# Attention two heads at a time, spread over the gate layer's blocks

## The chip, the cores and the metric

The kernel runs on one core of one Trainium2 chip. The time is device microseconds of one launch. The core has five engines with a queue each: TensorE (PE, matmuls; its weight loads are listed as PEld), VectorE (DVE), ScalarE (ACT), GpSimd (POOL) and SyncE (SP), which issues most of the DMAs. SBUF holds the tiles; matmuls write to PSUM, which has eight banks of 128 partitions x 512 fp32 values.

## What is computed

The reference is two blocks of a network over 512 positions of 1024 channels, one after the other. The first block mixes by spatial gating, a depthwise convolution and a pooling branch, and is not touched. The second block projects its normed input `h` to the inputs of two branches and two gates:

```python
proj = h @ w_in
qa, ka, va, za, ba, aa, qb, kb, vb, ga, gb = split(proj)
oa = gated_delta_rule(conv(qa), conv(ka), conv(va), ...)     # 4 heads of 128
ob = chunk_band_attention(qb, kb, vb, rel_bias)              # 8 heads of 64
mix = sigmoid(ga) * (oa @ w_branch_a) + sigmoid(gb) * (ob @ w_branch_b)
x = x + mix @ w_out
```

Attention is causal by chunks of 64 positions, with a bias by distance: for a head, `softmax(q @ k.T / 8 + bias) @ v`, where a query block of 128 positions sees its own block and those before it. So query blocks 0 to 3 have scores of 128 x 128, 256, 384 and 512.

## The kernel before

**Layout.** Activations stand transposed, channels on partitions and 512 positions along the row. A layer's weights come in blocks of 128 output channels, 512 KB each. `prep` (L149) loads a block on SP's queue and splits it into a high and a low part (`whi` by ACT, `wlo` by DVE); every product of a layer is three matmuls of 512 columns (`mm3`, L168 to L170), so a block of 1024 input channels takes 24. These are in a format that takes one pass. The small matmuls of attention and of the delta rule are plain fp32 and show as two instructions each in the trace, called passes here; transpositions show as one.

**Order.** `step` (L243) puts work in a list and `emit` (L246) issues it in that order, with weight blocks prepared two steps ahead. That is the order of the code, not of the engines: a planner (the tile framework) orders the instructions of each engine when the program is built. It goes through the program with a cost model of its own, and of what is ready by that model it sends first what stands first in the code; work from further down fills the time in which earlier work waits. Buffers are rings by tag: a tile waits until one of its ring's buffers is free. On the chip each engine then takes its list in order.

**The stage of the change** has PSUM banks "mm" 2, "g0" 2, "g1" 2 and "att" 2 (L766). Its steps, in the order of the code: the layer `w_za`, small gates, two delta-rule heads (`gdn_steps(0)` and `(1)`: three blocks of `w_qkv` each, then `gdn_first` and `gdn_second`), eight blocks of `w_qkb` (the attention's queries and keys, L1123), `w_vb` (its values, L1124), `step(attention)` (L1125), two more delta-rule heads (L1126, L1127), and 16 blocks of `w_gab`, the gate layer (L1128), whose results go to DRAM. After it `branches` (L1151) needs the outputs of all heads.

**Attention** goes over 8 heads, and in a head over three groups of query blocks, (0, 1), (2) and (3): 24 groups in one step. A tile of `S["at"]` holds two heads, the even one in partitions 0 to 63, the odd one in 64 to 127; `pr` is a head's half. `scores` (L1053) loads the head's bias in its first group, multiplies queries by keys with 64 rows of contraction (L1062) into one "att" bank, and makes the softmax on DVE and ACT in a tile `z` from the ring "az" of two. `values` (L1073) works on the group before: it transposes `z` by PE (L1080) into an "att" bank, copies that to a tile of the ring "ap" (two), multiplies by `vb` (L1086) into a third "att" tile, in the head's half of the output partitions, and copies the half to `ao`. When a pair of heads is complete, `ao` is split for the branches. The ring "g" of nine buffers (L854) holds query, key and value tiles of delta-rule heads, three a head, and later gate tiles.

Of the kernel before, what the change touches and what calls it, by code (L numbers as in the profile page):

```python
# [12 lines left out]
ALU = mybir.AluOpType  # L13
AX = mybir.AxisListType

P = 128
T = 512
D = 1024
NB = 8
NT = 4  # L20
# [6 lines left out]
DH_SCALE = 64 ** -0.5  # L27
# [16 lines left out]
def build(tc, d, out):  # L44
    nc = tc.nc
# [3 lines left out]
    pe = nc.tensor  # L49
# [8 lines left out]
    S = {}  # L58
# [26 lines left out]
    def blk(pool, tag, bufs, dt=F32, shape=(P, T)):  # L85
        return pool.tile(list(shape), dt, tag=tag, bufs=bufs, name=tag)
# [18 lines left out]
    def auxps(tag=None):  # L105
        tag = tag or PS["aux"]
        return PS["pool"].tile([P, T], F32, tag=tag, bufs=PS["banks"][tag], name=tag)
# [4 lines left out]
    def acopy(o, i, scale=1.0):  # L112
        act.activation(out=o, in_=i, func=AF.Copy, scale=scale)  # L113

    def tt(o, a, b, op):
        dve.tensor_tensor(out=o, in0=a, in1=b, op=op)  # L116

    def ts(o, a, s1, s2, op0, op1=None):
        if op1 is None:
            dve.tensor_scalar(out=o, in0=a, scalar1=s1, scalar2=None, op0=op0)  # L120
        else:
            dve.tensor_scalar(out=o, in0=a, scalar1=s1, scalar2=s2, op0=op0, op1=op1)

    def stt(o, a, s, b, op0, op1):
        dve.scalar_tensor_tensor(out=o, in0=a, scalar=s, in1=b, op0=op0, op1=op1)  # L125

    def split(src, hi, lo):
        acopy(hi, src)
        tt(lo, src, hi.bitcast(F32), ALU.subtract)
# [5 lines left out]
    def pair(set_):  # L135
        if set_ == "A":
            return blk(acts, "xh", 8, F32R), blk(acts, "xl", 8, F32R)
        return blk(acts, "th", 8, F32R), blk(acts, "tl", 8, F32R)
# [28 lines left out]
    def mm3(ps, wh, wl, xh, xl, first, last):  # L167
        pe.matmul(ps, wh, xh, start=first, stop=False)  # L168
        pe.matmul(ps, wh, xl, start=False, stop=False)  # L169
        pe.matmul(ps, wl, xh, start=False, stop=last)  # L170
# [72 lines left out]
    def step(fn, chunk=None, bg=2400, hold=None):  # L243
        steps.append((chunk, fn, bg, hold))
# [26 lines left out]
    def kchunks(kb):  # L271
        kmax = 8 if kb <= 8 else -(-kb // (-(-kb // 8)))
        return [(k0, min(kb, k0 + kmax)) for k0 in range(0, kb, kmax)]

    def linear(name, nbs, kb, xs, consume, bg=2400, tag="mm"):

        for n in nbs:
            st = {}
            for k0, k1 in kchunks(kb):
                def fn(wh, wl, n=n, k0=k0, k1=k1, st=st):  # L280
                    if k0 == 0:
                        st["ps"] = auxps(tag)
                    for k in range(k0, k1):
                        xh, xl = xs(k)
                        w = slice((k - k0) * P, (k - k0 + 1) * P)
                        mm3(st["ps"], wh[:, w], wl[:, w], xh, xl, k == 0, k == kb - 1)
                    if k1 == kb:
                        consume(n, st["ps"], ALL)

                step(fn, d[name][n][:, k0 * P:k1 * P], bg)  # L290
# [32 lines left out]
    def linear_tm(name, halves, kb, xs, consume, tag2, between=None):  # L323

        for hf in halves:
            st = {}
            cuts = [0, 1] if between is not None and hf == 0 else [0]
            cuts += list(range(2, kb + 1, 2))
            for k0, k1 in zip(cuts, cuts[1:]):
                def fn(wh, wl, hf=hf, k0=k0, k1=k1, st=st):  # L330
                    if k0 == 0:
                        st["ps"] = [mmps(), mmps(), auxps(tag2), auxps(tag2)]
                    for k in range(k0, k1):
                        xh, xl = xs(k)
                        c = slice((k - k0) * T, (k - k0 + 1) * T)
                        for tb in range(NT):
                            t = slice(tb * P, (tb + 1) * P)
                            ps = st["ps"][tb]
                            pe.matmul(ps, xh[:, t], wh[:, c], start=(k == 0), stop=False)  # L339
                            pe.matmul(ps, xh[:, t], wl[:, c], start=False, stop=False)  # L340
                            pe.matmul(ps, xl[:, t], wh[:, c], start=False, stop=(k == kb - 1))  # L341
                    if k1 == kb:
                        for tb in range(NT):
                            consume(hf, tb, st["ps"][tb])

                step(fn, d[name][hf][:, k0 * T:k1 * T])
                if between is not None and (hf, k1) == (0, 6):
                    step(between)
# [210 lines left out]
    z = [("w_z", n, 8, xa, pool_z) for n in range(NB)]  # L559
# [480 lines left out]
        S["vb"][tb] = blk(S["p2"], "at", 4)  # L1040
        acopy(S["vb"][tb], ps, S["Rtm"][:, tb:tb + 1])

    def attention():
        st = {}

        def spans(qbs):
            at = 0
            for qb in qbs:
                n = (qb + 1) * P
                yield qb, n, slice(at, at + n)  # L1050
                at += n

        def scores(h, qbs):  # L1053
            pr = slice((h % 2) * 64, (h % 2) * 64 + 64)
            q, k = S["at"][h // 2], S["at"][4 + h // 2]
            if qbs[0] == 0:
                st["bias"] = blk(S["p2"], "bias", 1)
                nc.sync.dma_start(st["bias"], d["bias"][h])
            ps = auxps("att")
            z = blk(S["p2"], "az", 2)  # L1060
            for qb, n, c in spans(qbs):
                pe.matmul(ps[:, c], q[pr, qb * P:n], k[pr, :n], start=True, stop=True)  # L1062
            for qb, n, c in spans(qbs):
                stt(z[:, c], ps[:, c], DH_SCALE, st["bias"][:, T - n:], ALU.mult, ALU.add)
                nm = tiny.tile([P, 1], F32, tag="nm", bufs=2, name="nm")
                sm = tiny.tile([P, 1], F32, tag="sm", bufs=2, name="sm")
                dve.reduce_max(out=nm, in_=z[:, c], axis=AX.X, negate=True)
                act.activation(out=z[:, c], in_=z[:, c], func=AF.Exp, bias=nm, accum_out=sm)
                dve.reciprocal(out=sm, in_=sm)
                ts(z[:, c], z[:, c], sm, None, ALU.mult)  # L1070
            return z

        def values(h, qbs, z):  # L1073
            pr = slice((h % 2) * 64, (h % 2) * 64 + 64)
            if h % 2 == 0 and qbs[0] == 0:
                st["ao"] = blk(S["p2"], "ao", 1)
            pt = auxps("att")
            m = sum(n for _, n, _ in spans(qbs))
            for c in range(0, m, P):
                pe.transpose(pt[:, c:c + P], z[:, c:c + P], ident)  # L1080
            pT = blk(S["p2"], "ap", 2)
            acopy(pT[:, :m], pt[:, :m])
            po = auxps("att")
            for i, (qb, n, c) in enumerate(spans(qbs)):
                for kb in range(qb + 1):
                    pe.matmul(po[pr, i * P:(i + 1) * P], S["vb"][kb][:, h * 64:(h + 1) * 64],  # L1086
                              pT[:, c.start + kb * P:c.start + (kb + 1) * P], start=(kb == 0), stop=(kb == qb))
            w = len(qbs) * P
            acopy(st["ao"][pr, qbs[0] * P:qbs[0] * P + w], po[pr, :w])
            if h % 2 == 1 and qbs[-1] == NT - 1:  # L1090
                hi, lo = S["A"][4 + h // 2] = pair("A")
                split(st["ao"], hi, lo)

        prev = None
        for h in range(8):
            for qbs in ((0, 1), (2,), (3,)):
                z = scores(h, qbs)
                if prev is not None:
                    values(*prev)
                prev = (h, qbs, z)  # L1100
        values(*prev)

    S["sd"] = [None] * 16

# [8 lines left out]
    def gdn_steps(hd):  # L1113
        gdn_qkv_steps(hd)
        step(lambda: gdn_first(hd))
        step(lambda: gdn_second(hd))
# [5 lines left out]
    for n in range(8):  # L1122
        linear("w_qkb", [n], 8, xb, att_qk, tag="mm" if n % 4 < 2 else "att")  # L1123
    linear_tm("w_vb", range(1), 8, xb, att_v, "att")  # L1124
    step(attention)  # L1125
    gdn_steps(2)  # L1126
    gdn_steps(3)  # L1127
    linear("w_gab", range(16), 8, xb, gates2)  # L1128

    def load_gate(i):  # L1130
        sg = blk(S["p2"], "g", 9)
# [208 lines left out]
def program(nc, arrays):  # L1340
    args = {
        name: nc.dram_tensor(f"in_{name}", a.shape, mybir.dt.from_np(a.dtype), kind="ExternalInput").ap()
        for name, a in arrays.items()
    }
    out = nc.dram_tensor("out_0", (NB, P, T), F32, kind="ExternalOutput").ap()
    with tile.TileContext(nc) as tc:
        build(tc, args, out)
# [13 lines left out]
```

## Time and profile before

| | us |
|---|---|
| median of three runs | 1835.45 |
| lowest and highest run | 1833.61, 1835.49 |
| profiled execution, its own time | 1834.4 |
| its span, first to last instruction | 1832.6 |
| PE busy | 1818.4 (99%) |
| DVE busy | 1182.4 (65%) |
| ACT busy | 750.5 (41%) |

The page shows one execution. Busy time of an engine is the time in which one of its instructions runs. A matmul's end is modelled, and matmuls follow each other before the one ahead has ended, so that a row's duration (0.39 us for 512 columns) is longer than the distance between two starts; the distance is what a matmul costs. The chain of waits follows the last instruction back to whatever released it.

### The profile page before, as it was taken

How to read it: one execution, taken by the hardware profiler on the slowest of the kernel's cores; microseconds unless marked ns; L12 is line 12 of the kernel's file. 1: busy time of each engine (PE TensorE's matmuls, PEld its weight loads, DVE VectorE, ACT ScalarE, POOL GpSimd, SP SyncE). 2: the span in 40 equal slices, each digit the busy share in tenths (PEclk: the TensorE clock that was granted, in tenths of full speed). 3: DMA queues.
4: the chain of work that ended last, by engine and by line, in shares of the span. 5: the costliest groups of instructions: out<-in, count | busy, mean ns of one | idle time of the engine just before them, and what ended most of it. 6: DMA issues, size and time to landing. Idle time of an engine off the chain costs nothing.

```text
span 1832.6 us, 22934 instructions
## 1 busy us (share of the span) xinstructions
PE 1818.4 (99%) x8932; PEld 1510.6 (82%) x8932; DVE 1182.4 (65%) x2050; ACT 750.5 (41%) x1233; POOL 0.7 (0%) x5
## 2 busy tenths in 40 slices
PE   9999999999999999999999999999999999999997
PEld 7888888888888888888897887777888888888887
DVE  7999968986458444442286784678636677777333
ACT  5442234326346232222254742686315444444221
POOL 0000000000000000000000000000000000000000
PEclk9999999999999999999999999999999999999999
DMA  6232223322343322323335122212245323232331
GB/s 202 94 115 92 93 87 99 114 92 81 111 166 115 100 96 94 102 87 98 103 133 175 59 64 86 75 30 75 99 149 190 128 96 100 93 103 90 95 96 66
DMA packets 62894, 189.73 MB, mean 104 GB/s; under 512 B 7233, under 2 KB 10433, under 8 KB 62785
## 3 DMA queue, kind: packets, MB, share of 16 engines
q1 hardware_dynamic: 56736, 177.53, 30.2%
q10 hardware_dynamic: 6048, 10.73, 1.8%
q8 instruction: 70, 1.15, 0.3%
q14 instruction: 40, 0.32, 0.1%
HBM read 176.70 MB, written 11.53 MB: 103 GB/s over the span
## 4 chain that ended last, share of the span: by engine, by line
PE 96%; DVE 2%; DMA 1%; ACT 1%; issue 0%; SPq 0%; DVEq 0%; ACTq 0%
PE mm L169 27%; PE mm L170 27%; PE mm L168 27%; PE att L1062 1%; PE att L1086 1%; PE g L982 1%; PE g L977 1%; PE att L170 1%; PE att L169 1%; PE att L168 1%; PE mm L340 1%; PE att L1080 1%; PE mm L341 1%; PE mm L339 1%; DVE wlo L116 1%; PE aux L216 1%
## 5 line engine op out<-in xcount | busy, mean ns | idle before, releaser
L113 ACT ACTIVATE whi<-raw 128x1024 fp32r<-128x1024 f32 (+3 forms) x304 | 312.3, 1027 | 657.6 <-PE mm L169 393.2
L116 DVE TENSOR_TENSOR wlo<-raw,whi 128x1024 fp32r<-128x1024 f32 (+3 forms) x304 | 359.0, 1182 | 194.0 <-ACT whi L113 191.4
L168 PE MATMUL mm<-xh,whi 128*128 128x512 f32 (+1 forms) x1032 | 393.7, 382 | 0.0
L169 PE MATMUL mm<-xl,whi 128*128 128x512 f32 (+1 forms) x1032 | 393.2, 381 | 0.0
L170 PE MATMUL mm<-xh,wlo 128*128 128x512 f32 (+1 forms) x1032 | 393.0, 381 | 0.0
L168 PE MATMUL mm<-th,whi 128*128 128x512 f32 (+1 forms) x976 | 379.0, 389 | 0.0
L169 PE MATMUL mm<-tl,whi 128*128 128x512 f32 (+1 forms) x976 | 378.7, 388 | 0.1
L170 PE MATMUL mm<-th,wlo 128*128 128x512 f32 (+1 forms) x976 | 378.5, 388 | 0.0
L170 PEld LDWEIGHTS mm<-xh,wlo 128*128 128x128 f32 x1032 | 194.0, 188 | 37.0
L169 PEld LDWEIGHTS mm<-xl,whi 128*128 128x128 f32 x1032 | 194.0, 188 | 37.0 <-issue 0.2
L168 PEld LDWEIGHTS mm<-xh,whi 128*128 128x128 f32 x1032 | 193.9, 188 | 37.1 <-issue 0.2
L169 PEld LDWEIGHTS mm<-tl,whi 128*128 128x128 f32 x976 | 183.7, 188 | 36.6 <-issue 1.6
L170 PEld LDWEIGHTS mm<-th,wlo 128*128 128x128 f32 x976 | 183.6, 188 | 36.0 <-issue 2.0
L168 PEld LDWEIGHTS mm<-th,whi 128*128 128x128 f32 x976 | 183.6, 188 | 35.9 <-issue 2.0
L125 DVE SCALAR_TENSOR_TENSOR cv<-hc,vec,cv 128x507 f32<-128x507 f32 (+18 forms) x240 | 172.4, 733 | 4.2 <-ACT cv L462 0.6
L170 PE MATMUL mm<-fh,wlo 128*128 128x512 f32 (+1 forms) x252 | 91.0, 361 | 0.0
L168 PE MATMUL mm<-fh,whi 128*128 128x512 f32 (+1 forms) x252 | 90.8, 360 | 0.0
L116 DVE TENSOR_TENSOR sg<-mm,R 128x512 f32<-128x512 f32 (+1 forms) x43 | 29.0, 677 | 89.7 <-PE mm L170 89.7
L169 PE MATMUL mm<-fl,whi 128*128 128x512 f32 (+1 forms) x236 | 84.6, 358 | 0.0
L116 DVE TENSOR_TENSOR t<-mm,R 128x512 f32<-128x512 f32 x56 | 38.5, 688 | 52.9 <-PE mm L170 51.0
L116 DVE TENSOR_TENSOR t<-mm,sg 128x512 f32<-128x512 f32 (+1 forms) x31 | 20.9, 673 | 62.6 <-PE mm L170 62.5
L168 PEld LDWEIGHTS mm<-fh,whi 128*128 128x128 f32 x252 | 47.6, 189 | 7.2
(375 smaller groups left out, 2079.9 us busy)
## 6 DMA issues: line engine op xcount, KB each, us to landing
raw<-in_w_ffn_in SPq DMA_DIRECT2D x44, 512.0 KB, 3.3
raw<-in_w_up SPq DMA_DIRECT2D x44, 512.0 KB, 3.3
raw<-in_w_g SPq DMA_DIRECT2D x24, 512.0 KB, 3.3
raw<-in_w_out SPq DMA_DIRECT2D x16, 512.0 KB, 3.4
raw<-in_w_ffn_out SPq DMA_DIRECT2D x16, 512.0 KB, 3.5
raw<-in_w_gab SPq DMA_DIRECT2D x16, 512.0 KB, 3.4
raw<-in_w_down SPq DMA_DIRECT2D x16, 512.0 KB, 3.5
raw<-in_w_qkv SPq DMA_DIRECT2D x12, 512.0 KB, 3.4
```

Of the source, the lines that this page charges most:

```text
L113: act.activation(out=o, in_=i, func=AF.Copy, scale=scale)
L116: dve.tensor_tensor(out=o, in0=a, in1=b, op=op)
L125: dve.scalar_tensor_tensor(out=o, in0=a, scalar=s, in1=b, op0=op0, op1=op1)
L168: pe.matmul(ps, wh, xh, start=first, stop=False)
L169: pe.matmul(ps, wh, xl, start=False, stop=False)
L170: pe.matmul(ps, wl, xh, start=False, stop=last)
L216: pe.matmul(r[:, b * P:(b + 1) * P], y[:, b:b + 1].to_broadcast([P, P]), ident, start=True, stop=True)
L339: pe.matmul(ps, xh[:, t], wh[:, c], start=(k == 0), stop=False)
L340: pe.matmul(ps, xh[:, t], wl[:, c], start=False, stop=False)
L341: pe.matmul(ps, xl[:, t], wh[:, c], start=False, stop=(k == kb - 1))
L977: pe.matmul(yp[:, B[b]], A[:, B[b]], Z[:, B[b]], start=True, stop=True)
L982: pe.matmul(zp[:, B[b]], Zt[:, B[b]], Y[:, B[b]], start=True, stop=True)
```

## The change

Attention now has 12 groups, four pairs of heads by three sets of query blocks. In a group both heads' score matmuls are issued in turn, query block by query block, each head in its half of the rows and into a bank of its own; then the softmax of one head and of the other. Both heads' scores are transposed and copied one after the other, and their value matmuls are issued in turn into one bank, each in its half of the output partitions, and copied out together. A group loads two biases when it is a pair's first; the second bias and the second `z` come from the ring "g". The single attention step goes; step `i` (the scores of group `i` and the values of group `i - 1`) stands ahead of block `i` of the gate layer, for `i` from 0 to 12, behind all delta-rule heads.

```diff
+    TWO = [slice(0, 64), slice(64, P)]
+    st = {}
+
+    def scores(j, qbs):
+
+        q, k = S["at"][j], S["at"][4 + j]
+        if qbs[0] == 0:
+            st["bias"] = [blk(S["p2"], *x) for x in (("bias", 1), ("g", 9))]
+            for e in range(2):
+                nc.sync.dma_start(st["bias"][e], d["bias"][2 * j + e])
+        ps = [auxps("att") for _ in TWO]
+        zs = [blk(S["p2"], *x) for x in (("az", 2), ("g", 9))]
+        for qb, n, c in spans(qbs):
+            for e, pr in enumerate(TWO):
+                pe.matmul(ps[e][:, c], q[pr, qb * P:n], k[pr, :n], start=True, stop=True)
+        for e, z in enumerate(zs):
             for qb, n, c in spans(qbs):
-                pe.matmul(ps[:, c], q[pr, qb * P:n], k[pr, :n], start=True, stop=True)
-            for qb, n, c in spans(qbs):
-                stt(z[:, c], ps[:, c], DH_SCALE, st["bias"][:, T - n:], ALU.mult, ALU.add)
+                stt(z[:, c], ps[e][:, c], DH_SCALE, st["bias"][e][:, T - n:], ALU.mult, ALU.add)
...
+    def values(j, qbs, zs):
+
+        if qbs[0] == 0:
+            st["ao"] = blk(S["p2"], "ao", 1)
+        m = sum(n for _, n, _ in spans(qbs))
+        pts = []
+        for z in zs:
             pt = auxps("att")
-            m = sum(n for _, n, _ in spans(qbs))
             for c in range(0, m, P):
                 pe.transpose(pt[:, c:c + P], z[:, c:c + P], ident)
...
+            pts.append(blk(S["p2"], "ap", 2))
+            acopy(pts[-1][:, :m], pt[:, :m])
+        po = auxps("att")
+        for i, (qb, n, c) in enumerate(spans(qbs)):
+            for kb in range(qb + 1):
+                for e, pr in enumerate(TWO):
+                    h = 2 * j + e
                     pe.matmul(po[pr, i * P:(i + 1) * P], S["vb"][kb][:, h * 64:(h + 1) * 64],
...
+                              pts[e][:, c.start + kb * P:c.start + (kb + 1) * P], start=(kb == 0), stop=(kb == qb))
+        w = len(qbs) * P
+        acopy(st["ao"][:, qbs[0] * P:qbs[0] * P + w], po[:, :w])
+        if qbs[-1] == NT - 1:
+            hi, lo = S["A"][4 + j] = pair("A")
+            split(st["ao"], hi, lo)
+
+    GROUPS = [(j, qbs) for j in range(4) for qbs in ((0, 1), (2,), (3,))]
+
+    def attention(i):
+        zs = scores(*GROUPS[i]) if i < len(GROUPS) else None
+        if i:
+            values(*GROUPS[i - 1], st["zs"])
+        st["zs"] = zs
...
-    step(attention)
     gdn_steps(2)
     gdn_steps(3)
-    linear("w_gab", range(16), 8, xb, gates2)
+    for n in range(16):
+        if n <= len(GROUPS):
+            step(lambda i=n: attention(i))
+        linear("w_gab", [n], 8, xb, gates2)
```

## Rows read from the trace of the kernel before

**Rows 1.** The page's head: the span, the busy times, PE's granted clock in 40 slices, and the shares of the chain that ended last.

```profile
span 1832.6 us, 22934 instructions
...
PE 1818.4 (99%) x8932; PEld 1510.6 (82%) x8932; DVE 1182.4 (65%) x2050; ACT 750.5 (41%) x1233; POOL 0.7 (0%) x5
...
PEclk9999999999999999999999999999999999999999
...
PE 96%; DVE 2%; DMA 1%; ACT 1%; issue 0%; SPq 0%; DVEq 0%; ACTq 0%
```

**Rows 2.** Busy time by stretches. Columns: the stretch (us from the span's start), its length, then busy us and number of instructions of PE, PEld, DVE, ACT and POOL, the granted clock, the DMA share, GB/s.

```profile
1151.00:1275.00 124.00, 123.46 (x696) 90.17 (x694) 93.27 (x263) 91.60 (x223) 0.00 (x0) 1.00 0.19 58
1275.00:1330.00 55.00, 54.76 (x316) 44.74 (x316) 34.89 (x80) 17.23 (x48) 0.00 (x0) 1.00 0.29 95
1330.00:1371.00 41.00, 41.00 (x183) 33.95 (x182) 14.75 (x16) 8.49 (x8) 0.00 (x0) 1.00 0.41 143
```

**Rows 3.** The view of the tile `att`: line, engine, operation, tiles and number, then duration in ns (least, median, most), the first and the last start, and the forms.

```profile
L1086 PE MATMUL att<-ap,at x160: 272/273/324, 1157.7 to 1274.5; 128*64 128x128 f32 x160
...
L1080 PE MATMUL att<-ident,az x80: 270/272/331, 1155.8 to 1272.6; 128*128 128x128 f32 x80
...
L1062 PE MATMUL att<-xl,xh x64: 272/430/693, 1151.5 to 1266.1; 64*128 64x128 f32 x16, 64*128 64x256 f32 x16, 64*128 64x384 f32 x16, 64*128 64x512 f32 x16
...
L125 DVE SCALAR_TENSOR_TENSOR az<-att,bias x32: 281/482/693, 1152.4 to 1266.7; 128x128 f32<-128x128 f32 x8, 128x256 f32<-128x256 f32 x8, 128x384 f32<-128x384 f32 x8, 128x512 f32<-128x512 f32 x8
...
L168 PE MATMUL att<-xh,whi x32: 389/389/389, 1372.0 to 1412.1; 128*128 128x512 f32 x32
```

**Rows 4.** The timeline of PE and PEld inside attention: start (us), duration (us), engine, line, operation, tiles, shape and number of instructions that follow each other; in brackets the idle time before, and what ended it. L1086 are values, L1062 scores, L1080 transpositions, L168 to L170 a layer's matmuls.

```profile
1157.10 0.40 PE L170 MATMUL mm<-th,wlo 128*128 128x512 f32 x1
...
1157.33 0.40 PE L168 MATMUL mm<-th,whi 128*128 128x512 f32 x1
1157.66 0.63 PEld L1086 LDWEIGHTS att<-ap,at 128*64 128x64 f32 x6 [0.37 <-ACT ap L113]
1157.66 0.87 PE L1086 MATMUL att<-ap,at 128*64 128x128 f32 x6
...
1158.46 1.12 PE L1062 MATMUL att<-xl,xh 64*128 64x512 f32 x2
...
1159.51 0.55 PE L1080 MATMUL att<-ident,az 128*128 128x128 f32 x3
...
1159.82 0.47 PE L169 MATMUL mm<-tl,whi 128*128 128x512 f32 x1
...
1160.13 0.39 PE L170 MATMUL mm<-th,wlo 128*128 128x512 f32 x1
...
1161.48 0.92 PE L1062 MATMUL att<-xl,xh 64*128 64x128 f32 x4
...
1162.33 0.51 PE L169 MATMUL mm<-tl,whi 128*128 128x512 f32 x1
...
1162.67 0.40 PE L170 MATMUL mm<-th,wlo 128*128 128x512 f32 x1
```

**Rows 5.** The same view, a group with eight value passes and scores of 384 columns.

```profile
1164.58 1.09 PE L1086 MATMUL att<-ap,at 128*64 128x128 f32 x8
1165.60 0.91 PE L1062 MATMUL att<-xl,xh 64*128 64x384 f32 x2
1166.44 0.50 PE L170 MATMUL mm<-th,wlo 128*128 128x512 f32 x1
```

**Rows 6.** PE's timeline in a delta-rule head: eight passes of 64 rows by 64 columns, and the layer's matmul behind them.

```profile
1259.64 0.67 PE L993 MATMUL g<-GZ,Gdec 64*64 64x64 f32 x8
1260.25 0.50 PE L169 MATMUL mm<-tl,whi 128*128 128x512 f32 x1
```

**Rows 7.** From the view of the tile `az`, columns as in rows 3: the softmax's maximum on DVE.

```profile
L1067 DVE TENSOR_REDUCE nm<-az x32: 275/476/686, 1152.9 to 1267.9; 128x1 f32<-128x128 f32 x8, 128x1 f32<-128x256 f32 x8, 128x1 f32<-128x384 f32 x8, 128x1 f32<-128x512 f32 x8
```

**Rows 8.** PE's timeline at two places: a layer's matmul with scores behind it, and a layer's matmul that follows values, with what comes after it.

```profile
1151.13 0.39 PE L168 MATMUL mm<-th,whi 128*128 128x512 f32 x1
1151.45 1.56 PE L1062 MATMUL att<-xl,xh 64*128 64x128 f32 x6
...
1270.38 0.50 PE L168 MATMUL mm<-th,whi 128*128 128x512 f32 x1
1270.71 0.38 PE L1004 MATMUL g<-Gdec,g 128*128 128x128 f32 x2
```

**Rows 9.** The view of the tile `bias`: its DMAs with the durations of the issue, who waited for them (us, times), and the time from issue to landing.

```profile
L1058 SPq DMA_DIRECT2D bias<-in_bias x8: 327/328/423, 984.6 to 1250.3; - x8
...
  DVE az L125: 1.3, 1
...
DMA to landing us min/median/max: 2.5/2.6/3.9
```

**Rows 10.** PE's timeline in the stretch with gate blocks alone.

```profile
1340.06 0.39 PE L168 MATMUL mm<-th,whi 128*128 128x512 f32 x1
...
1340.29 0.39 PE L169 MATMUL mm<-tl,whi 128*128 128x512 f32 x1
```

**Rows 11.** The view of line 1031, the last transpositions of each delta-rule head, columns as in rows 3.

```profile
L1031 PE MATMUL g<-ident,Ggam x16: 270/274/328, 1095.1 to 1323.6; 128*128 128x128 f32 x16
```

**Rows 12.** PE's timeline at the longest idle time that a transposition has ahead of it.

```profile
1223.74 0.63 PE L1080 MATMUL att<-ident,az 128*128 128x128 f32 x4 [0.54 <-ACT whi L113]
```

More of the change, by code (lines that the diff above doesn't have):

```diff
@@ L1041, in att_v, with spans @@
         acopy(S["vb"][tb], ps, S["Rtm"][:, tb:tb + 1])
[L1043 to L1060, printed above, removed]
+    def spans(qbs):
+        at = 0
+        for qb in qbs:
+            n = (qb + 1) * P
+            yield qb, n, slice(at, at + n)
+            at += n
+    TWO = [slice(0, 64), slice(64, P)]
[12 more added lines that the diff above has]
+        for e, z in enumerate(zs):
             for qb, n, c in spans(qbs):
-                pe.matmul(ps[:, c], q[pr, qb * P:n], k[pr, :n], start=True, stop=True)
-            for qb, n, c in spans(qbs):
-                stt(z[:, c], ps[:, c], DH_SCALE, st["bias"][:, T - n:], ALU.mult, ALU.add)
+                stt(z[:, c], ps[e][:, c], DH_SCALE, st["bias"][e][:, T - n:], ALU.mult, ALU.add)
                 nm = tiny.tile([P, 1], F32, tag="nm", bufs=2, name="nm")
@@ L1070, in scores @@
                 ts(z[:, c], z[:, c], sm, None, ALU.mult)
[L1071 to L1076, printed above, removed]
+        return zs
+    def values(j, qbs, zs):
[4 more added lines that the diff above has]
+        for z in zs:
             pt = auxps("att")
-            m = sum(n for _, n, _ in spans(qbs))
@@ L1079, in values @@
             for c in range(0, m, P):
                 pe.transpose(pt[:, c:c + P], z[:, c:c + P], ident)
[L1081 to L1085, printed above, removed]
-                    pe.matmul(po[pr, i * P:(i + 1) * P], S["vb"][kb][:, h * 64:(h + 1) * 64],
-                              pT[:, c.start + kb * P:c.start + (kb + 1) * P], start=(kb == 0), stop=(kb == qb))
@@ L1088, in values @@
[L1088 to L1101, printed above, removed]
+            pts.append(blk(S["p2"], "ap", 2))
```

## Prediction

> **What bounds the kernel now.** I read the page first. TensorE (PE) is busy 1818.4 of 1832.6 us, the chain of waits is 96% PE, and the granted clock is full in every slice [rows 1]. So the time is the sum of what PE does, one thing after the other, and an edit pays only by what it takes off PE, or costs by what it makes PE wait. Then the table by stretches, for the part that the change reorders: attention with the filler around it (1151 to 1275), the rest of the delta-rule heads (1275 to 1330), gate blocks alone (1330 to 1371): 220 us, in which PE is not busy for 0.8 us [rows 2]. VectorE and ScalarE have room (143 and 117 of 220 us). The planner has already filled every wait of attention with matmuls of other layers. The view by tile gives the pieces: 64 score passes, 160 value passes, 80 transpositions [rows 3]. Two passes stand for one fp32 matmul.
>
> "Busy" hides one thing, which the PE timeline shows when starts are subtracted [rows 4, 5]. Inside a run, a gate-layer matmul of 512 columns takes 0.23 us (1157.10 to 1157.33). A value pass takes 0.11: eight take 1.02, six take 0.80. A score pass takes 0.105 per 128 columns: two of 512 take 1.05, two of 384 take 0.84. But PE loses time where it goes from one shape of the array to another. The matmul ahead of values takes 0.33 in place of 0.23 (0.10 lost); six value passes should take 0.66 and take 0.80 (0.14); a score run takes 0.21 over its passes (1.05 against 0.84 for 512; 0.85 against 0.63 for 128 and 256); the matmul behind scores takes 0.34 (0.11). A group of today goes full array, values, scores, full array: 0.10 + 0.14 + 0.21 + 0.11 = 0.56 us, but 0.51 where transpositions come next (1159.51 to 1160.13, 0.62 for 3 x 0.11 + 0.23). About 0.53, and 24 groups: 12.8 us of 1835.
>
> **The change part by part.** (1) *Scores of two heads in turn.* Columns streamed are the same: 8 heads x 2 passes x (1+2+3+4) x 0.105 = 16.8 us. New is that neighbours in PE's queue lie in different halves of the rows. No row of before has two such neighbours, so the gain is bounded: nothing if passes run one after the other, half if two heads run as one. The nearest row is a run of 64x64 matmuls, eight at 0.61 us, 0.076 each with its entry and exit [rows 6]: a quarter of the array works no faster than its columns, so a smaller piece alone gains nothing, only a neighbour in a free half could. Between the ends I take this: the two passes of a head use the same half and stay in line, while the second pass of one head runs beside the first pass of the other. Then every change of head saves one pass: for the pair of query blocks (0, 1) 0.105 + 0.105 + 0.21 = 0.42, for block 2 0.315, for block 3 0.42, so 1.155 for two heads and 4.6 us for four pairs. Ends: 0 and 8.4.
>
> (2) *Values of two heads in turn*, each into its half of the output columns: 160 x 0.11 = 17.6 us today. By the same reasoning a run of 12 passes takes 7 and one of 16 takes 9: 5 + 5 + 7 = 17 passes saved for a pair, 1.87 us, 7.5 in all. That wants both heads' transposed scores ready at once. I don't expect it: there are two "att" banks, the scores hold both, and the second head's bank comes free only after VectorE's step on it, up to 0.69 us after the first, with a reduction of 0.69 that may come between [rows 3, 7]; meanwhile PE has 0.23 us matmuls to go on with. So the first value matmul goes ahead alone, its fellows wait for the second head's copy (same bank, so I take them to keep their order), and the saving is 4 + 4 + 6 = 14 passes, 1.54 us for a pair, 6.2 in all. Ends: 0 and 8.8.
>
> (3) *Changes of array shape.* 12 groups in place of 24. Scores between full-array matmuls cost 0.09 (1151.13 to 1151.45 is 0.32) + 0.21 + 0.11 = 0.41; values 0.10 + 0.14 + 0.10 (1270.38 to 1270.71 is 0.33) = 0.34 [rows 4, 5, 8]. Today values and scores touch, since one bank frees both. With the scores of a step placed behind the gate block before, I take them apart: 0.75 a group, 9.0 in all. The value matmul that goes ahead adds 0.34: 1.09, 13.1 in all. So this gives back 12.8 - 13.1 = -0.3 in my case; +3.8 if values stay whole, +6.1 if they also touch the scores (0.56 x 12 = 6.7).
>
> (4) *The move.* Attention passes behind the last two delta-rule heads, into steps ahead of gate blocks 0 to 12. Its matmuls, softmax steps and copies are the same in number of columns (12 copies into `ao` go, off the path). The eight bias loads go with it past the `w_qkv` loads on SP's queue; they land in 2.6 us, and one held VectorE for 1.3 us today [rows 9]; now two come per pair, a gate block ahead. The second bias and the second `z` come from the "g" ring: heads 2 and 3 hold six of nine, three are left, enough. I cost the move at nothing. The cover is the gate layer, 16 blocks x 24 x 0.227 = 87 us in the quiet stretch [rows 10]. The last values stand ahead of block 12, with four blocks, 22 us, to hide one group's chain. The delta-rule heads, which today end at 1323 against branches that start at 1372.0, come earlier [rows 3, 11]. Uncovered, each wait would cost what rival 3 says.
>
> Sum: -4.6 - 6.2 + 0.3 = -10.5. The profiled execution took 1834.4 us around its span of 1832.6; that gives 1823.9. The median shown is 1835.45, so the forecast against it is 1824.9 us.
>
> The Trainium skill ("TensorE: Matmul & The Clock Gate", Part 3, measured speedup) gives 3.07 times for four row pieces and 2.38 for three column pieces; an estimate from that page for two (77 and 79% of full: 1.54 and 1.59) would make parts (1) and (2) 5.9 and 6.5 us, and the sum -12.1; no row here shows it.
>
> **The rivals.** *1. The halves don't overlap at all.* Every like run in the trace keeps one pass per pass time, and no row shows otherwise. Then only part (3) is left: -0.3 to +6.1 saved, 1829.3 to 1835.7, with scores and values apart and whole 1831.6, with the split 1835.7; middle 1833. For it: no evidence of overlap in the trace. Against: nothing but that the halves share neither rows nor output.
>
> *2. Only the scores overlap.* The value passes of both heads load over all 128 rows, and if the load for one half must wait for the matmul of the other, or if the planner sends one head's values whole and then the other's, part (2) is 0. -4.6 + 0.3 = -4.3: 1831.1. Against it: six value loads take 0.63 us under matmuls of 0.87 today, in one half [rows 4]. The same page of the Trainium skill (Part 3, what overlaps and what doesn't) says that weight loads run beside matmuls only where row groups differ, which would give this rival's time; the row with six hidden loads does not agree with it for the half that is in use, and no run here shows two halves.
>
> *3. Slower: PE's queue waits for the two "att" banks.* A step now wants five tiles of them, scores twice, transpositions twice, values. PE takes its queue in order. Where the planner puts the second head's transpositions or the values too early, PE stands still. Today's instance: 0.54 us idle ahead of a transposition, with everything else behind it [rows 12]. If in each of 12 steps both waited for one VectorE step of 0.69, that is 24 x 0.69 = 16.6 us: -10.5 + 16.6 = +6.1, 1841.5. No gain from 0.44 us a wait, slower by over 0.2% from 0.59. Against: 48 like waits of today leave 0.54 us idle in 124 [rows 2].
>
> **How the numbers follow.** Forecast case (both overlap, passes of a head in line): 0.50, its own range 1819 (no value matmul ahead: -4.6 - 7.5 - 3.8 = -15.9) to 1829 (4 us of it eaten by waits as in rival 3). Rival 1: 0.18. Rival 2: 0.17. Rival 3: 0.12. Overlap beyond my model (both heads as one, 8.4 + 8.8 saved): 0.03. The largest saving with shape changes whole is -4.6 - 7.5 - 6.1 = -18.2: 1817. Range 1817 to 1835.7, which holds the forecast case, rival 2 and rival 1, and leaves out rival 3 and the last case. 0.2% (3.7 us) is about what a measurement of this kernel can tell; faster than that is below 1831.8. Faster: 0.50 + 0.03 + 0.12 of rival 2 + 0.03 of rival 1 = 0.68; same: 0.05 + 0.13 + 0.02 of rival 3 = 0.20; slower 0.12.
>
> **What would show it.** On the changed kernel's PE timeline: starts of two heads' score passes closer than 0.105 per 128 columns, four passes of 512 in about 1.3 us and not 1.7 (part 1); a run of value passes at about 0.055 each (part 2), and whether one matmul goes ahead of it; the number of places where the 0.23 us matmul takes 0.33 (part 3); no idle PE ahead of transpositions and branches (part 4). If PE's starts keep today's distances inside all runs, rival 1 is right; if only the scores draw together, rival 2; if PE's idle time in the stage grows by more than 5 us, rival 3.

## The result, and the profile after

The changed kernel takes 1824.91 us (median of four runs, 1824.26 to 1826.73) against 1835.47 (1833.61 to 1835.66) for the one before: a ratio of 0.9946, interval 0.9929 to 0.9964. The forecast was 1824.9. The sum came out; two of its terms did not, and they made up for each other, as the experiments show.

The head of the page of the changed kernel, as in [rows 1]:

```profile
span 1824.9 us, 22886 instructions
...
PE 1807.8 (99%) x8932; PEld 1501.4 (82%) x8932; DVE 1183.0 (65%) x2050; ACT 740.6 (41%) x1217; POOL 0.7 (0%) x5
...
PE 94%; DVE 3%; ACT 1%; DMA 1%; issue 1%; SPq 0%; DVEq 0%; ACTq 0%
```

PE has as many instructions as before and is busy 10.6 us less: the same matmuls take less time. Its share of the chain fell from 96 to 94%, DVE's and issue's rose: a little of the gain became waiting.

The view of the tile `att` after (columns as in [rows 3]; L1093 are the values, L1064 the scores, L1085 the transpositions of one head and of the other, L168 the branches; the last line is idle time ahead of these rows that ended with DVE's step on `az`, us and times, the queues of matmuls and of weight loads added):

```profile
L1093 PE MATMUL att<-ap,at x160: 272/273/324, 1223.3 to 1339.4; 128*64 128x128 f32 x160
...
L1064 PE MATMUL att<-xl,xh x64: 272/481/693, 1192.6 to 1327.0; 64*128 64x128 f32 x16, 64*128 64x256 f32 x16, 64*128 64x384 f32 x16, 64*128 64x512 f32 x16
...
L1085 PE MATMUL att<-ident,az x40: 270/273/328, 1221.2 to 1336.3; 128*128 128x128 f32 x40
...
L1085 PE MATMUL att<-ident,g x40: 270/272/328, 1221.5 to 1336.8; 128*128 128x128 f32 x40
...
L168 PE MATMUL att<-xh,whi x32: 389/389/389, 1363.3 to 1403.5; 128*128 128x512 f32 x32
...
  DVE az L125: 5.0, 11
```

The counts are those of [rows 3], and the least and the longest durations all but the same, but the branches start at 1363.3 in place of 1372.0. No row of a single instruction shows the gain; it is in the distances. PE's timeline over one group after:

```profile
1297.78 0.39 PE L170 MATMUL mm<-th,wlo 128*128 128x512 f32 x1
1298.10 1.13 PE L1064 MATMUL att<-xl,xh 64*128 64x512 f32 x4
1299.16 0.50 PE L168 MATMUL mm<-th,whi 128*128 128x512 f32 x1
1299.50 0.39 PE L169 MATMUL mm<-tl,whi 128*128 128x512 f32 x1
...
1300.19 0.39 PE L169 MATMUL mm<-tl,whi 128*128 128x512 f32 x1
1300.95 0.55 PE L1085 MATMUL att<-ident,az 128*128 128x128 f32 x3 [0.37 <-DVE az L125]
...
1302.23 0.43 PE L1093 MATMUL att<-ap,at 128*64 128x128 f32 x2
1302.59 0.50 PE L169 MATMUL mm<-tl,whi 128*128 128x512 f32 x1
...
1304.64 0.87 PE L1093 MATMUL att<-ap,at 128*64 128x128 f32 x10
1305.44 0.50 PE L168 MATMUL mm<-th,whi 128*128 128x512 f32 x1
```

Four score passes of 512 columns take 1.06 us (1298.10 to 1299.16); two took 1.05 before [rows 4]. Both heads run as one. Ten value passes take 0.80, what six took. One value matmul, two passes, goes ahead by itself at 1302.23. And the matmul at 1300.19 stands 0.76 us ahead of the next start where 0.23 is usual: PE waits for DVE to empty the score bank.

To see where the stage's time went I added the distances between PE's starts by kind, from the first matmul behind `w_vb` to the first matmul of the branches, in this trace and in those of the experiments (us):

| | before | after | scores in one half | values in one half | second head first | old place | neither overlaps | place alone |
|---|---|---|---|---|---|---|---|---|
| scores | 21.7 | 13.4 | 20.1 | 13.4 | 13.4 | 18.9 | 20.3 | 21.8 |
| values | 20.9 | 14.5 | 14.5 | 21.2 | 10.5 | 14.7 | 21.2 | 21.5 |
| transpositions | 8.0 | 8.2 | 7.8 | 8.6 | 7.5 | 8.5 | 8.2 | 7.2 |
| delta-rule heads | 36.6 | 38.0 | 37.3 | 38.2 | 37.6 | 36.9 | 38.0 | 37.8 |
| layers' matmuls | 133.7 | 136.8 | 134.6 | 136.8 | 135.7 | 135.4 | 134.1 | 135.1 |
| stage | 220.9 | 210.9 | 214.3 | 218.3 | 204.7 | 214.4 | 221.9 | 223.4 |

A wait of PE's shows in the row of the matmul ahead of it. Scores give 8.3 us and values 6.5; 4.8 come back in the other three rows.

### The profile page after: what moved, and what is told of

Same layout as the page of the kernel before. It is cut to its first block, busy times and chain, and to the rows that moved or that the text cites. A ratio compares the mean times of both kernels' runs of the same rounds, so it can differ in the third digit from the quotient of the medians.

```text
span 1824.9 us, 22886 instructions
## 1 busy us (share of the span) xinstructions
PE 1807.8 (99%) x8932; PEld 1501.4 (82%) x8932; DVE 1183.0 (65%) x2050; ACT 740.6 (41%) x1217; POOL 0.7 (0%) x5
## 3 DMA queue, kind: packets, MB, share of 16 engines
q8 instruction: 70, 1.15, 0.3%
## 4 chain that ended last, share of the span: by engine, by line
PE 94%; DVE 3%; ACT 1%; DMA 1%; issue 1%; SPq 0%; DVEq 0%; ACTq 0%
PE mm L169 27%; PE mm L168 27%; PE mm L170 27%; PE g L977 1%; PE g L982 1%; PE att L1093 1%; DVE wlo L116 1%; ACT whi L113 1%; PE mm L340 1%; PE mm L341 1%; PE att L170 1%; PE att L168 1%; PE att L169 1%; PE mm L339 1%; PE att L1085 1%
## 5 line engine op out<-in xcount | busy, mean ns | idle before, releaser
L168 PE MATMUL mm<-xh,whi 128*128 128x512 f32 (+1 forms) x1032 | 393.7, 382 | 0.0
L170 PE MATMUL mm<-xh,wlo 128*128 128x512 f32 (+1 forms) x1032 | 393.0, 381 | 0.0
L168 PE MATMUL mm<-th,whi 128*128 128x512 f32 (+1 forms) x976 | 379.7, 389 | 0.4 <-ACT th L113 0.4
L170 PE MATMUL mm<-th,wlo 128*128 128x512 f32 (+1 forms) x976 | 378.0, 387 | 0.0
L170 PEld LDWEIGHTS mm<-xh,wlo 128*128 128x128 f32 x1032 | 193.9, 188 | 37.2
L168 PEld LDWEIGHTS mm<-xh,whi 128*128 128x128 f32 x1032 | 193.9, 188 | 37.2 <-issue 0.2
L169 PEld LDWEIGHTS mm<-xl,whi 128*128 128x128 f32 x1032 | 194.0, 188 | 36.9 <-issue 0.2
L168 PEld LDWEIGHTS mm<-th,whi 128*128 128x128 f32 x976 | 183.5, 188 | 39.4 <-issue 4.6
L169 PEld LDWEIGHTS mm<-tl,whi 128*128 128x128 f32 x976 | 183.6, 188 | 36.6 <-issue 1.9
L170 PEld LDWEIGHTS mm<-th,wlo 128*128 128x128 f32 x976 | 183.6, 188 | 35.2 <-issue 1.2
L170 PE MATMUL mm<-fh,wlo 128*128 128x512 f32 (+1 forms) x252 | 91.0, 361 | 0.0
L168 PE MATMUL mm<-fh,whi 128*128 128x512 f32 (+1 forms) x252 | 90.8, 360 | 0.0
L116 DVE TENSOR_TENSOR t<-mm,sg 128x512 f32<-128x512 f32 (+1 forms) x31 | 20.9, 673 | 62.5 <-PE mm L170 62.5
L168 PEld LDWEIGHTS mm<-fh,whi 128*128 128x128 f32 x252 | 47.6, 189 | 7.2
```

## The experiments

Theory A: two halves of the array work at the same time, and that is the gain. Rival B: the gain is the fewer changes of shape. Rival C: it is the new place. All numbers are against the kernel before on the same chip.

**1. Scores in one half.**

```diff
-                pe.matmul(ps[e][:, c], q[pr, qb * P:n], k[pr, :n], start=True, stop=True)
+                pe.matmul(ps[e][:, c], q[:64, qb * P:n], k[:64, :n], start=True, stop=True)
```

> The changed kernel, with the score matmuls of both heads taken from the rows of the first head's half, so both lie in one half of the array (the second head's scores are then made from the first head's queries and keys). PE's order, shapes and number of matmuls are the same. Theory A (two neighbours in different halves run as one): about 7.1 us of paired score passes come back, 8.4 for all less two places where PE's order leaves a score matmul alone; 1832, and starts 7 ns apart vanish from the scores. Rival B (the gain is in fewer changes of array shape, and the close starts are only how starts are stamped): 1825, no change.

Measured 1829.23 us, 0.9970 (0.9958 to 0.9981), 0.24% of the time above the change. PE's timeline of this kernel, the same group:

```profile
1300.25 1.98 PE L1064 MATMUL att<-xl,xh 64*128 64x512 f32 x4
1302.16 0.50 PE L168 MATMUL mm<-th,whi 128*128 128x512 f32 x1
...
1303.19 0.39 PE L169 MATMUL mm<-tl,whi 128*128 128x512 f32 x1
1303.42 0.49 PE L1085 MATMUL att<-ident,az 128*128 128x128 f32 x3
```

The four passes take 1.91 us, not 1.06: rival B falls, for PE's order and shapes are the same. But the kernel lost 4.3 us where its scores lost 6.7. The rest is in the last row but one: the wait ahead of the transpositions is gone (1303.19 to 1303.42 is 0.23). In the whole stage PE is idle for 0.24 us, and for 1.98 in the change, with the matmuls in the same order by their starts. So some of what overlapping scores win, PE spends waiting for DVE behind them. How much is less sure: 6.7 - 4.3 = 2.4 us by the medians, 3.3 by the stages of the two traces (214.3 - 210.9 = 3.4 us lost).

**2. Values in one half.**

```diff
+        w = len(qbs) * P
...
-                    pe.matmul(po[pr, i * P:(i + 1) * P], S["vb"][kb][:, h * 64:(h + 1) * 64],
-                              pts[e][:, c.start + kb * P:c.start + (kb + 1) * P], start=(kb == 0), stop=(kb == qb))
-        w = len(qbs) * P
-        acopy(st["ao"][:, qbs[0] * P:qbs[0] * P + w], po[:, :w])
+                    pe.matmul(po[:64, e * w + i * P:e * w + (i + 1) * P], S["vb"][kb][:, h * 64:(h + 1) * 64],
+                              pts[e][:, c.start + kb * P:c.start + (kb + 1) * P], start=True, stop=True)
+        for e, pr in enumerate(TWO):
+            acopy(st["ao"][pr, qbs[0] * P:qbs[0] * P + w], po[:64, e * w:e * w + w])
```

> The changed kernel, with the value matmuls of both heads written to the same half of the output partitions, in different columns, each for itself instead of summed over key blocks; two copies of a half in place of one of the whole. Number, shape and turn of the matmuls stay. Theory A: 58 value passes that today run beside another come back, 58 x 0.109 = 6.3 us: 1831. Rival B: 1825. If only row halves overlap and the values' gain is of another kind, 1825 too.

Measured 1832.32, 0.9988 (0.9979 to 0.9996). PE's timeline:

```profile
1308.56 1.31 PE L1094 MATMUL att<-ap,at 128*64 128x128 f32 x10
1309.80 0.50 PE L168 MATMUL mm<-th,whi 128*128 128x512 f32 x1
```

Ten passes take 1.24 us, not 0.80. Column halves overlap as row halves do. PE's order is not quite that of the change, though: values come in 26 visits to their shape and not in 23. By estimate the three entries are 0.4 us (3 x 0.14) of the 6.7 by which the row of the values grows; 58 passes of 0.109 make the other 6.3.

**3. Neither overlaps**, both edits together.

> The changed kernel with both heads' scores in one half of the rows and both heads' values in one half of the columns, as in the first two experiments together: groups, place and order of the change, no two halves beside each other. Theory A: all gain goes, 1824.9 + 4.3 + 7.4 = 1836.6. If fewer groups and changes of shape, or the place, hold a part of it: 1829 to 1833.

Measured 1836.86, 1.0006 (0.9997 to 1.0015): the whole gain is gone, to within the interval. PE's timeline of this kernel:

```profile
1305.20 1.98 PE L1064 MATMUL att<-xl,xh 64*128 64x512 f32 x4
1307.11 0.50 PE L168 MATMUL mm<-th,whi 128*128 128x512 f32 x1
...
1311.98 1.30 PE L1094 MATMUL att<-ap,at 128*64 128x128 f32 x10
1313.22 0.50 PE L168 MATMUL mm<-th,whi 128*128 128x512 f32 x1
```

Twelve groups in place of 24, and the new place, are worth nothing together. (Values come in 26 visits here too.)

**4. Two heads at a time in the old place.**

```diff
+    for n in range(len(GROUPS) + 1):
+        step(lambda i=n: attention(i))
     gdn_steps(2)
     gdn_steps(3)
     for n in range(16):
-        if n <= len(GROUPS):
-            step(lambda i=n: attention(i))
         linear("w_gab", [n], 8, xb, gates2)
```

> The changed attention, two heads at a time, as steps in the old place ahead of the last two delta-rule heads, not spread over the gate blocks. Theory A (overlap and shapes make the gain, the place nothing): 1823 to 1827. Rival C (the place makes a good part of it): 1829 to 1834.

Measured 1829.26, 0.9972 (0.9961 to 0.9982): half the gain is gone, on rival C's side. The table says where: scores take 18.9 us, not 13.4; values are as in the change. PE's and then ACT's timeline of this kernel:

```profile
1177.88 0.87 PE L1093 MATMUL att<-ap,at 128*64 128x128 f32 x10
1178.68 1.73 PE L1064 MATMUL att<-xl,xh 64*128 64x512 f32 x4
```

```profile
1178.85 0.38 ACT L113 ACTIVATE ao<-att 128x256 f32<-128x256 f32 x1 [0.80 <-PE att L1093]
```

Here groups run close behind each other, and scores directly follow values. The second "att" bank holds the values until ACT has copied them, to 1179.23. The first head's passes start at 1178.68 and 1179.22, the second head's at 1179.29 and 1179.82: the second head comes one pass late, so only its first pass runs beside the first head's second, four passes in some 1.7 us. In the change a gate block lies between, both banks are free when the scores start, and their starts lie 0.007 us apart.

**5. The place alone**: one head at a time as before, two groups a gate block; `one(i)` makes the scores of group `i` and the values of group `i - 1`.

```diff
-    step(attention)
     gdn_steps(2)
     gdn_steps(3)
-    linear("w_gab", range(16), 8, xb, gates2)
...
+    for n in range(16):
+        for i in (2 * n, 2 * n + 1):
+            if i <= len(GROUPS):
+                step(lambda i=i: one(i))
+        linear("w_gab", [n], 8, xb, gates2)
```

> The kernel before, one head at a time, with its 24 groups as steps ahead of the gate blocks (two a block), behind all delta-rule heads: the change's place without its pairs. Theory A with the addition that e4 asks for (the place pays only because both score banks are then free, so that heads can run side by side): nothing, 1833 to 1837. Rival C (the place gains by itself, through better filling): 1831.

Measured 1837.67, 1.0016 (1.0007 to 1.0025), some 3 us slower. So rival C falls as a gain of its own: in these runs the place pays only through the overlap of scores. It costs something by itself: entries into the value shape rise from 24 to 28, and layers' matmuls and delta-rule heads take 1.4 and 1.2 us more.

**6. The second head's values first.**

```diff
-                for e, pr in enumerate(TWO):
+                for e, pr in ((1, TWO[1]), (0, TWO[0])):
```

> The changed kernel, with the second head's value matmul ahead of the first head's in each turn, so that the first of a group waits for the copy that comes last and none goes ahead alone. Theory A: 22 more passes run beside another (2.4 us) and 11 fewer excursions into the value shape (0.34 each, 3.7 us): 1818.8. Rival B (shape changes only): 1821. If the waiting then leaves PE without work: 1825 or more.

Measured 1818.87, 0.9918 (0.9904 to 0.9931), the best here together with experiments 8 and 10. PE's timeline of this kernel:

```profile
1296.44 0.55 PE L1085 MATMUL att<-ident,az 128*128 128x128 f32 x3 [0.37 <-DVE az L125]
...
1299.78 0.88 PE L1093 MATMUL att<-ap,at 128*64 128x128 f32 x12
1300.59 0.50 PE L169 MATMUL mm<-tl,whi 128*128 128x512 f32 x1
```

Twelve passes take 0.81 us, what six take alone: full overlap, and one visit to the value shape a group in place of two.

**7. One head's values after the other's**, with the loop over heads outermost.

```diff
-        for i, (qb, n, c) in enumerate(spans(qbs)):
-            for kb in range(qb + 1):
-                for e, pr in enumerate(TWO):
+        for e, pr in enumerate(TWO):
+            for i, (qb, n, c) in enumerate(spans(qbs)):
+                for kb in range(qb + 1):
```

> The changed kernel with one head's value matmuls issued whole, then the other's, each in its own half of the output partitions as in the change; only the turn goes. Theory A (only direct neighbours run together, so a run of 3 and 3 has one pair at its middle): 40 passes more than the changed kernel, 4.4 us, less some 7 excursions into the value shape that fall together, 2.4 us: 1827. If halves overlap without being next to each other: 1822.

Measured 1827.85, 0.9964 (0.9951 to 0.9978), near the 1827 for direct neighbours. But the reason is not quite that. PE's timeline of this kernel:

```profile
1266.41 1.14 PE L1093 MATMUL att<-ap,at 128*64 128x128 f32 x12
1267.49 0.50 PE L168 MATMUL mm<-th,whi 128*128 128x512 f32 x1
```

Six passes of one half and then six of the other take 1.08 us. With one pair of matmuls at the middle they would take 0.14 + 10 x 0.11 = 1.24. More than the direct neighbours met. In this run, and in the one at 1232.65, ACT had copied both heads' operands before the run began, and the second half's first pass starts 0.275 us in, beside the third of the first half's six: four passes met. In the runs of twelve that take 1.15 to 1.21 us it starts later, 0.05 us after ACT's copy for that head has ended. So the second half does not wait for the first one's end, but it also does not begin with it, as in experiment 6 (0.81).

**8. Transpositions in other banks**, on top of 6.

```diff
-            pt = auxps("att")
+            pt = auxps(f"g{len(pts)}")
```

> The changed kernel with the second head's value matmul first, as before, and the transposed scores in banks g0 and g1 in place of att, so that transpositions don't wait for VectorE to empty the score banks. Theory S (the planner counts the two heads' scores one after the other, so PE comes to the transpositions too early and stands): the waits ahead of transpositions go, about 3 us less than 1818.9, 1816. Rival: the waits move to another place, or the delta-rule heads miss the banks: 1818 to 1822.

Measured 1818.83, 0.9913 (0.9899 to 0.9926): the same as 6. The stage in the table of stretches, kernel 6 and then this one (columns as in [rows 2]):

```profile
1151.10:1355.90 204.80, 202.87 (x1194) 157.95 (x1193) 143.91 (x359) 108.87 (x263) 0.00 (x0) 1.00 0.26 91
```

```profile
1151.10:1355.20 204.10, 203.28 (x1193) 159.27 (x1192) 144.16 (x359) 108.99 (x263) 0.00 (x0) 1.00 0.27 91
```

PE's idle time falls from 1.93 to 0.82 us and the layers' matmuls from 135.7 to 133.1, so the waits were in good part the score banks'. But scores rise from 13.4 to 16.1 and transpositions from 7.5 to 8.5: the planner now sends more of the scores singly, and in four groups the second head starts late. One cost takes the other's place.

**9 and 10**, both on top of 8. In 9 the values stand ahead of the next scores in the step, with their sums in "g0"; in 10 their sums lie in "g1". Both leave "att" to the scores.

> As the last, and with the values of a group ahead of the next group's scores in the step, and the values' sums in a g0 bank: transpositions, scores and values then stand next to each other in PE's order in most groups, and both att banks are free for scores. Fewer changes of shape (some 10 groups x 0.2 to 0.4) on top of theory S: 1813 to 1815. If PE now waits for ScalarE's copies of the transposed scores, 0.5 us a group: 1819 or more.

> The changed kernel with the second head's value matmul first, transposed scores in banks g0 and g1, values in g1: the two att banks are left to the scores alone. In the kernel with only the transpositions moved, PE's idle time fell by 1.1 us but scores took 16.1 us in place of 13.4, since the planner sent more of them singly. Theory A with S: scores back to 13.4, idle time stays low: 1816. Rival: the banks of the delta-rule heads are missed until these end and attention backs up behind them: 1819 or more.

Measured 1819.50, 0.9919 (0.9906 to 0.9933), and 1819.00, 0.9913 (0.9900 to 0.9927). Neither beats 6. Scores take 17.4 and 15.4 us: with the "att" banks free the planner still sends many single scores while delta-rule heads run. So the 13.4 expected for 10 and the 1813 to 1815 for 9 both fell; what would keep the scores together in that stretch was not tried, and whether the waits named for 1819 are the cause is not shown.

## Why the prediction came out, point by point

**What bounds the kernel** was right: PE full, the time a sum of distances; experiments 1 to 3 take away overlap on PE, and the time follows.

**(1) Scores, -4.6.** The mechanism held; the size failed at the step "the two passes of a head use the same half and stay in line, while the second pass of one head runs beside the first pass of the other". In the change, the first passes of both heads start 0.007 us apart, and so do the second ones: four passes of 512 take 1.06 us with their entry, where I named about 1.3 without it. So the gain is near the other end: 6.7 us by experiment 1, 8.4 if every group met its neighbour (two groups early in the stage did not). Both heads as one is the case that I gave a chance of 0.03. What I assumed does happen in experiment 4, where the second head waits for its bank.

**(2) Values, -6.2.** Right in size and in its main step. In 11 of 12 groups one value matmul goes alone, in ten of them ahead of its fellows, and the rest overlaps. Measured by experiment 2: 6.7 us in the row of the values, 7.4 us of time. The step that failed in (1) was wrong here as well, twelve passes taking six pass times and not seven (experiment 6), but behind a matmul that goes ahead both rules give the same. The rule on weight loads of the Trainium skill that stands beside rival 2 ("TensorE: Matmul & The Clock Gate", Part 3, what overlaps and what doesn't) does not hold for these runs: value halves share all rows, and ten passes take 0.80 us where one half takes 1.24. The speedups that the Trainium skill measured (the same Part 3, measured speedup) gave 5.9 and 6.5 us by estimate and lie near the 6.7 and 6.7 measured.

**(3) Changes of shape, +0.3.** Near: the change has 15 visits to the scores' shape and 23 to the values', where I counted 12 and 24. Experiment 3, which keeps groups and place and takes the overlap away, is 1.0006 (0.9997 to 1.0015), but it holds this term and the move together, and no run parts them. I priced the split at 7.5 - 6.2 = 1.3 us of passes and 0.3 + 3.8 = 4.1 of shape; ahead of experiment 6 it was 2.4 + 3.7, and taking the split away gained 6 us by the medians.

**(4) The move, nothing.** This step failed, both ways. For single heads the place costs about 3 us (experiment 5); for pairs it brings about 4 (change against experiment 4), since both score banks are then free when the scores start. The delta-rule heads did end earlier (last transposition at 1271.4 in place of 1323.6), and bias loads held nobody. "No idle PE ahead of transpositions" was wrong: DVE's emptying of the score banks held transpositions in 11 places, with the queue of weight loads idle for 3.9 us (7 places) and that of matmuls for 1.2 us (4). Much of the first lies under matmuls still running, so the 5.0 us of the view is not time lost. Rival 3's mechanism is there in small: PE's idle time in the stage rose from 0.78 to 1.98 us, and distances ahead of transpositions grew. Experiment 1 prices what scores' overlap gives back there at 2.4 us by the medians. PE's matmuls start in the same order in the change and in experiment 1, so the planner's order does not depend on the overlap; that it is early for that reason is how I read it.

So scores brought some 2 us more than forecast, values half a us, and waits, put at nothing, took about as much back: the total is right to 0.1 us by chance, the direction by reasoning. Rival 1 fell by experiments 1 to 3, rival 2 by experiment 2. The waits, some 2.4 us in all, stayed far under rival 3's 0.44 us for each of 24, 10.6 us.

## What to carry to other kernels

Small fp32 matmuls with 64 rows or 64 output columns are worth issuing in turns, one for each half, since two took the time of one here. Both operands and both banks must be ready at the same moment, so let the first of a pair be the one that is ready last (6 us in experiment 6). Look at distances between starts, not at durations: those of single matmuls stayed all but the same while the time of a pair halved. After such an edit, look behind it: the engine comes early to its next wait, and here that took back a third to a half of what the scores' overlap won.

## What was not expected of the hardware

- The halves behave as if each worked off a line of its own, up to a limit. Two passes of one head and two of the other, head by head in the code, start as pairs 0.007 us apart (change). Twelve value passes, six and six in the code, take 1.08 to 1.21 us, less than the 1.24 that one meeting at the middle would give (experiment 7), but at most four passes of the first half met the second. The traces give starts, not the order in PE's queue, so the mechanism is not shown.
- A run costs what its longer half costs: 10 passes, six and four, took 0.80, as six alone and as twelve (0.81).
- Overlap was complete: four passes of 512 columns in 1.06 us against 1.05 for two, with the rows of both halves read at once; and twelve value passes in 0.81 against six in 0.80, with a different moving operand for each column half.
